# The written order of a decoder layer: output projection and first gate, the slots' steps, the down product's place, and the closing sums

## The chip, the cores and the metric

The kernel runs on one core of one Trainium2 chip. The metric is the device time of one execution in microseconds (us). The kernel before takes 1375.45 us, the median of three executions that lie between 1373.59 and 1375.83. All times below are in us where nothing else is said.

A core has five engines that each run their own queue of instructions in order: TensorE (PE in the profile; PEld is its weight loads), VectorE (DVE), ScalarE (ACT), GpSimd (POOL), and SyncE (SP), which here issues DMA transfers. They wait for each other through semaphores. An instruction that waits holds up everything behind it on its own engine.

## The reference

One post-norm decoder layer on x of 1024 tokens by 1024 columns, all in float32:

```python
mod = silu(c) @ w_mod + b_mod              # shift, scale, gate, twice
h   = x * (1 + scale1) + shift1
mix = hybrid_mixer(h, w_in, w_pool, pool_scale, w_o)
x   = layer_norm(ALPHA * x + gate1 * mix, ln1_g, ln1_b)
h   = x * (1 + scale2) + shift2
ffn = (silu(h @ w_gate) * (h @ w_up)) @ w_down      # D_FF = 2816
x   = layer_norm(ALPHA * x + gate2 * ffn, ln2_g, ln2_b)
```

`hybrid_mixer` projects h, runs eight heads of sparse top-k attention and a causal pooling of 512 channels, sets both beside each other and multiplies by `w_o`. The change touches nothing up to that product. It begins with `... @ w_o`, and reaches to the end: first layer norm, feed-forward part, second layer norm.

## The kernel before, in words

**Split products.** A float32 operand is held as a high half (a copy rounded to the matmul's type fp32r, made by ScalarE) and a low half (the operand less its high half, a subtraction on VectorE or GpSimd). A product is three matmuls, high by high, high by low, and low by high (`SPLITS`). So a matmul may wait for a copy on ScalarE, and the second or third in a row for the subtraction behind it. In the text "low" is that subtraction.

**Output projection.** Tokens stand in eight tiles of 128 (`XR[7]` to `XR[0]`, tiles `res_X` in the trace: tile t at offset 1024*t). For each tile TensorE makes `wo` products, VectorE reads them out onto the residual (`wo_evac`) and takes the statistics of the layer norm, and ScalarE applies it. `region_t(t)` then transposes the tile on TensorE (`xT`), and ScalarE (for the last tiles VectorE in part) applies scale and shift while it copies the transposed blocks to a stage (`stage_W`). Two tiles make one of four regions: region 0 is tiles 7 and 6, region 3 is 1 and 0. `region_sums` makes four differences of blocks per region, T3 on GpSimd, the others on VectorE; `region_split` makes high halves (ScalarE) and low halves (VectorE or GpSimd, `REGION_G`) in `hr_H`, the tokens as the feed-forward products take them. `affine(t)` multiplies the normalized tile by the gain row and adds the bias row on GpSimd, four steps of 128x512, for the residual. In this stage the steps of the four engines are placed by a scheduler from costs; the table `MID` says behind which half of which tile's products each region step is written. From `region_t(2)` on the order is as written ("pinned").

**Feed-forward.** The 2816 columns go in 11 pairs of 256 (`NFP` = 11). Gate, up and down products are each done by a Strassen-like scheme: seven products on 2x2 blocks instead of eight, steps g0 to g6, u0 to u6, d0 to d6. A step is twelve matmuls of 128x512 (`gu` or `dn` in the trace). Its weight block is prepared on GpSimd (`block_prep`: gain products or differences of raw blocks `wraw_R`, `wraw_W`), copied high by ScalarE (`block_high`) and given its low half (`block_low`) by VectorE, or by GpSimd in the slots that `LOW_G` names. There are four block buffers (`wblk_V6144`, `wblk_V7168`, `wblk_T0`, `wblk_T1024`); the copy for the step three ahead is written in this step's slot, its low half one slot later. In the loop over pairs p = 1 to 10 the steps of gate and up of pair p and of down of pair p-1 take turns as `DOWN_AT` says; the last pair has no down steps. The two last pairs' down products are done in a closing part without the scheme.

Up steps end in the product of gate and up, blocks A11 (final after u4), A12, A22 (u6), and from these the differences S1 to S4: `act_W4096` is A11, `act_R2048` is S1, each with high and low half. `utmp_X` and `gtmp_V` hold them in float32. Down steps read them in the order A11, A12, S1, A22, S3, S4, S2; each ends in four sums onto the residual (`res_X<-res_X,dn`) on VectorE.

**What sets the order of a slot.** `slot(sl)` is called once per step, behind the matmuls of step `sl`. It writes, for the step before: the sums and products on VectorE (`prev.vec()`); the lows of block copies (`all_low()`); the lows of activations (`lows`); the differences (`prev.sums()`); preparation of blocks on GpSimd; the copies on ScalarE; and the copy of `sl` itself. Each engine runs its share in this order.

**The end.** The scheme keeps the residual in combined parts; twelve "returns" (`turn`: a sum of two 128x512 parts) undo that in the last pair, on GpSimd but for one (`RETURN_AT`). Behind them stand the gain products of the last two pairs' eight down blocks. Closing: for each tile in `ORDER`, four blocks by three matmuls per half, one sum on VectorE per half, the layer norm, and the output DMA.

All engine calls go through one helper, so nearly every row of the trace shows line L164 of the kernel before (L169 of the changed one); tiles tell the places apart.

## Time and profile before

| | |
|---|---|
| median of three executions | 1375.45 |
| profiled execution, its own time | 1372.83 |
| its span in the trace | 1371.0 |
| mean granted clock of TensorE | 0.938 |
| TensorE matmul busy | 1209.9 (88%) |
| TensorE weight loads busy | 946.9 (69%) |
| VectorE busy | 1055.0 (77%) |
| ScalarE busy | 610.2 (45%) |
| GpSimd busy | 841.3 (61%) |
| DMA, mean over the span | 76 GB/s |

The profiled execution is one execution, not one of the three; span and rows are its own. A row of the timeline or of grouped instructions gives the time from the span's start, the time from the first start to the last end, the engine, the operation, output tiles and input tiles by name, the shape, and the count; in brackets at its end stands the idle time of the engine just before the row and what ended it. The page and the helper leave buffer numbers out of names. Where a mean clock is given it is the share of full speed that TensorE was granted in that stretch.

The stages in the trace: the `wo` products run up to about 640, the first pair's gate and up from there to about 720, then nine pairs with down steps, of which eight are alike, from 722 to about 1270; the last pair and the closing part fill the rest.

### The profile page before, as it was taken

What the parts mean: (1) busy time and instruction counts of PE and PEld (TensorE: products, weight loads), DVE (VectorE), ACT (ScalarE), POOL (GpSimd) and SP (SyncE); (2) the same over time, 40 slices, a digit from 0 to 9 for tenths busy, and PEclk for the clock granted to TensorE, in tenths of its full rate; (3) what the DMA queues carried; (4) which work ended last, traced back from release to release, by engine and by line L of the source; (5) the groups of instructions that cost most, each with busy time, mean ns of one, the idle gap of its engine ahead of it and who ended that gap; (6) DMA issues with size and microseconds to landing.
All of it is one profiled execution on the core that took longest, in us unless ns stands there. A gap on an engine that the chain in (4) does not pass through costs nothing.

```text
span 1371.0 us, 16162 instructions
## 1 busy us (share of the span) xinstructions
PE 1209.9 (88%) x5462; PEld 946.9 (69%) x5462; DVE 1055.0 (77%) x1722; ACT 610.2 (45%) x1149; POOL 841.3 (61%) x790
## 2 busy tenths in 40 slices
PE   7989996778668997997799999999999999999976
PEld 6656575656536654785777787878787787878865
DVE  6898899899988787576687767586777767585678
ACT  3446633545656776346534333343433333342421
POOL 1492774857434456249747767686767767685847
PEclk9999998979869998998999999999999999999988
DMA  9630020301100366400111111201011111202112
GB/s 328 242 139 16 16 92 16 123 16 47 39 16 9 93 207 231 161 24 16 58 58 35 58 62 47 77 31 62 31 63 36 57 62 47 77 32 92 59 50 108
DMA packets 34904, 103.91 MB, mean 76 GB/s; under 512 B 3843, under 2 KB 3843, under 8 KB 33286
## 3 DMA queue, kind: packets, MB, share of 16 engines
q1 hardware_dynamic: 34822, 102.88, 21.7%
q8 instruction: 43, 0.70, 0.2%
q14 instruction: 39, 0.32, 0.1%
HBM read 93.42 MB, written 9.45 MB: 75 GB/s over the span
## 4 chain that ended last, share of the span: by engine, by line
PE 36%; DVE 10%; POOL 3%; issue 2%; ACT 1%; DVEq 0%; POOLq 0%; ACTq 0%
PE gu L164 23%; PE dn L164 14%; DVE utmp_X L164 3%; DVE act_W L164 2%; DVE gtmp_V L164 1%; DVE act_R L164 1%; POOL res_X L164 1%; DVE wblk_T L164 1%; DVE wblk_V L164 1%; POOL wraw_R L164 1%; POOL wraw_W L164 1%; POOL hr_H L164 0%; DVE stat_C L164 0%; DVE res_X L164 0%; DVE hr_H L164 0%
## 5 line engine op out<-in xcount | busy, mean ns | idle before, releaser
L164 PE MATMUL gu<-hr_H,wblk_V 128*128 128x512 f32 (+1 forms) x936 | 225.3, 394 | 15.1 <-DVE wblk_V L164 14.4
L164 PE MATMUL gu<-hr_H,wblk_T 128*128 128x512 f32 (+1 forms) x912 | 218.7, 393 | 11.6 <-DVE wblk_T L164 10.6
L164 PEld LDWEIGHTS gu<-hr_H,wblk_V 128*128 128x128 f32 x936 | 177.1, 193 | 53.9 <-DVE wblk_V L164 16.5
L164 PEld LDWEIGHTS gu<-hr_H,wblk_T 128*128 128x128 f32 x912 | 172.4, 193 | 48.3 <-DVE wblk_T L164 12.3
L164 DVE TENSOR_TENSOR res_X<-res_X,dn 128x512 f32<-128x512 f32 (+1 forms) x253 | 163.5, 680 | 46.1 <-PE dn L164 46.0
L164 PE MATMUL pj<-ws_W,hT_H 128*128 128x512 f32 x456 | 125.5, 425 | 18.7 <-DVE kr_K L164 6.5
L164 PEld LDWEIGHTS pj<-ws_W,hT_H 128*128 128x128 f32 x456 | 89.6, 203 | 46.4 <-issue 16.6
L164 POOL TENSOR_TENSOR wraw_R<-wraw_R 128x512 f32<-128x512 f32 x64 | 93.5, 1467 | 12.9 <-DVE wblk_T L164 6.9
L164 POOL TENSOR_SCALAR sm_H<-sm_H,stat_X 128x1024 f32<-128x1024 f32 (+7 forms) x64 | 58.2, 922 | 70.0 <-DVE stat_X L164 53.4
L164 POOL TENSOR_TENSOR wraw_W<-wraw_W 128x512 f32<-128x512 f32 x60 | 87.9, 1468 | 17.5 <-DVE wblk_T L164 12.9
L164 DVE TENSOR_TENSOR gtmp_V<-gtmp_V,gu 128x512 f32<-128x512 f32 (+1 forms) x47 | 29.7, 650 | 67.7 <-PE gu L164 34.3
L164 PE MATMUL dn<-wblk_T,act_W 128*128 128x512 f32 x336 | 80.8, 392 | 0.0
L164 DVE TENSOR_SCALAR_CACHE_REDUCE junk_X<-keysD_T,colsD_X 128x1024 int16<-128x1024 int16 (+1 forms) x64 | 78.9, 1270 | 0.8
L164 PE MATMUL dn<-wblk_V,act_W 128*128 128x512 f32 x312 | 74.5, 390 | 0.0
L164 PEld LDWEIGHTS dn<-wblk_T,act_W 128*128 128x128 f32 x336 | 64.0, 190 | 13.6
L164 POOL TENSOR_TENSOR wblk_T<-wraw_W,wblk_T 128x512 fp32r<-128x512 f32 x29 | 41.8, 1444 | 44.2 <-ACT wblk_T L164 44.1
L164 PEld LDWEIGHTS dn<-wblk_V,act_W 128*128 128x128 f32 x312 | 58.9, 189 | 12.4
L164 DVE TENSOR_TENSOR utmp_X<-utmp_X,gu 128x512 f32<-128x512 f32 x33 | 22.5, 681 | 57.4 <-ACT utmp_X L164 57.4
L164 POOL TENSOR_TENSOR wblk_T<-wraw_R,wblk_T 128x512 fp32r<-128x512 f32 x29 | 42.4, 1463 | 36.8 <-ACT wblk_T L164 36.5
L164 POOL TENSOR_TENSOR colsA_X<-colsA_X 128x1 f32<-128x1 f32 (+1 forms) x124 | 33.3, 277 | 49.5 <-ACT junkA_T L164 39.0
L164 ACT ACTIVATE wblk_V<-wraw_R 128x512 fp32r<-128x512 f32 x55 | 34.7, 631 | 64.8 <-POOL wraw_R L164 30.4
L164 ACT ACTIVATE wblk_T<-wraw_W 128x512 fp32r<-128x512 f32 x55 | 34.6, 630 | 63.2 <-POOL wraw_W L164 24.0
(300 smaller groups left out, 2873.4 us busy)
## 6 DMA issues: line engine op xcount, KB each, us to landing
wm_K<-in_wma_dram SPq DMA_DIRECT2D x16, 512.0 KB, 10.2
modraw_V<-in_wmc_dram SPq DMA_DIRECT2D x16, 512.0 KB, 4.6
...
```

The lines of the kernel that those rows point to most:

```text
L164: ins_ = f(*a, **k)
```

## The change

One table per decision is changed, and the stage of output projection and first gate is written out by hand.

1. `DOWN_AT` starts a pair with d0 ahead of g0, g1, g2 and ends it with u2 to u6.
2. `slot` takes the order of its three VectorE parts from `SLOT_ORDER` ("b" lows of blocks, "a" lows of activations, "s" differences), and `early` (`COPY_AT`) can put the step's own copy at four places.
3. `LOW_G` names other slots; 46 lows go from GpSimd to VectorE over the kernel. `ACT_G` gives the low of S2 instead of S3 to GpSimd. `FIRST_G` gives the lows of six slots of the first pair to GpSimd.
4. From the first `wo_evac` on the order is as written: readouts and norms of 7, 6, 5 and 4 in turn, each tile's products as a generator (`wo_tile`) between whose halves transposes, differences and splits stand. Of the affine steps those of tiles 4 and 3 go to the slots of the first pair (`mults`, `adds` have ten entries instead of six).
5. The end: six returns are named in the last but one and the last pair and six behind the closing sums of tiles 6 and 5; blocks of the closing part are prepared earlier (`PREP_ON`, `may_make`); for the first two tiles of `ORDER` the half of the closing sums that needs the last but one pair only is written first (`last_down` with `(0, 1)`).

**Boundary of two pairs, TensorE** (one of the steady boundaries; the first row of each list is u6; `wblk` is the weight block, `act_W4096` is A11, `act_W2048` is A12). Before:

```order
L164 MATMUL gu_398_6739<-hr_H0_2677,wblk_V7168_4095 128x512 x12
L164 MATMUL gu_404_6867<-hr_H0_2677,wblk_T0_4096 128x512 x12
L164 MATMUL dn_405_6892<-wblk_T1024_4097,act_W4096_4104 128x512 x3
L164 MATMUL dn_406_6893<-wblk_T1024_4097,act_W4096_4104 128x512 x3
L164 MATMUL dn_407_6894<-wblk_T1024_4097,act_W4096_4104 128x512 x3
L164 MATMUL dn_408_6895<-wblk_T1024_4097,act_W4096_4104 128x512 x3
L164 MATMUL gu_409_6918<-hr_H0_2677,wblk_V6144_4094 128x512 x12
L164 MATMUL gu_404_6867<-hr_H0_2677,wblk_V7168_4095 128x512 x12
```

and now:

```order
L169 MATMUL gu_398_6739<-hr_H0_2677,wblk_V7168_4095 128x512 x12
L169 MATMUL dn_404_6867<-wblk_T0_4096,act_W4096_4104 128x512 x3
L169 MATMUL dn_405_6868<-wblk_T0_4096,act_W4096_4104 128x512 x3
L169 MATMUL dn_406_6869<-wblk_T0_4096,act_W4096_4104 128x512 x3
L169 MATMUL dn_407_6870<-wblk_T0_4096,act_W4096_4104 128x512 x3
L169 MATMUL gu_408_6898<-hr_H0_2677,wblk_T1024_4097 128x512 x12
L169 MATMUL gu_409_6918<-hr_H0_2677,wblk_V6144_4094 128x512 x12
L169 MATMUL gu_408_6898<-hr_H0_2677,wblk_V7168_4095 128x512 x12
```

d0, in both cases four groups of three matmuls on `act_W4096`, now stands right behind u6 (`gu_398` on `wblk_V7168`), ahead of the next pair's g0.

**Same place, VectorE** (from the low half of A11 on). Before:

```order
L164 TENSOR_TENSOR act_W4096_4104<-gtmp_V4096_4111,act_W4096_4104 128x512
L164 TENSOR_TENSOR utmp_X8704_4116<-utmp_X8704_4116,gu_398_6739 128x512
L164 TENSOR_TENSOR gtmp_V4608_4112<-gtmp_V4608_4112,utmp_X8704_4116 128x512
L164 TENSOR_TENSOR act_R2048_4108<-utmp_X8192_4115,act_R2048_4108 128x512
L164 TENSOR_TENSOR utmp_X8192_4115<-utmp_X8192_4115,gtmp_V4096_4111 128x512
L164 TENSOR_TENSOR utmp_X8704_4116<-utmp_X8192_4115,gtmp_V4608_4112 128x512
L164 TENSOR_TENSOR wblk_V7168_4095<-wraw_W0_4103,wblk_V7168_4095 128x512
L164 TENSOR_TENSOR res_X7168_4080<-res_X7168_4080,dn_405_6892 128x512
```

and now:

```order
L169 TENSOR_TENSOR act_W4096_4104<-gtmp_V4096_4111,act_W4096_4104 128x512
L169 TENSOR_TENSOR utmp_X8704_4116<-utmp_X8704_4116,gu_398_6739 128x512
L169 TENSOR_TENSOR gtmp_V4608_4112<-gtmp_V4608_4112,utmp_X8704_4116 128x512
L169 TENSOR_TENSOR wblk_V6144_4094<-wraw_W0_4103,wblk_V6144_4094 128x512
L169 TENSOR_TENSOR act_R2048_4108<-utmp_X8192_4115,act_R2048_4108 128x512
L169 TENSOR_TENSOR utmp_X8192_4115<-utmp_X8192_4115,gtmp_V4096_4111 128x512
L169 TENSOR_TENSOR utmp_X8704_4116<-utmp_X8192_4115,gtmp_V4608_4112 128x512
L169 TENSOR_TENSOR res_X7168_4080<-res_X7168_4080,dn_404_6867 128x512
```

Before, the only block low in this stretch is that of g2 (`wblk_V7168`), behind the low of S1 (`act_R2048`) and the two differences into `utmp_X`; that of g1 was GpSimd's. Now g1's (`wblk_V6144`) is here, ahead of those three, and g2's isn't, and d0's sums (`res_X`) stand directly behind the differences.

**Output projection, GpSimd** (`stage_W4096<-stage_W6144` is region difference T3, `hr_H` the low halves of a region, `res_X` with `gr_G` or `lnb_R` an affine step). Before:

```order
L164 TENSOR_TENSOR res_X6144_4079<-res_X6144_4079,lnb_R2048_4272 128x512
L164 TENSOR_TENSOR hr_H0_2677<-stage_W4096_4092,hr_H0_2677 128x512 x3
L164 TENSOR_TENSOR hr_H0_2677<-stage_W6144_4093,hr_H0_2677 128x512
L164 TENSOR_TENSOR hr_H0_2677<-stage_W4096_4092,hr_H0_2677 128x512
L164 TENSOR_TENSOR res_X5120_4078<-res_X5120_4078,gr_G0_76 128x512 x2
L164 TENSOR_TENSOR res_X5120_4078<-res_X5120_4078,lnb_R2048_4272 128x512 x2
L164 TENSOR_TENSOR res_X4096_4077<-res_X4096_4077,gr_G0_76 128x512 x2
L164 TENSOR_TENSOR res_X4096_4077<-res_X4096_4077,lnb_R2048_4272 128x512 x2
L164 TENSOR_TENSOR stage_W4096_4092<-stage_W6144_4093 128x512
```

and now:

```order
L169 TENSOR_TENSOR stage_W4096_4092<-stage_W6144_4093 128x512
L169 TENSOR_TENSOR hr_H0_2677<-stage_W6144_4093,hr_H0_2677 128x512
L169 TENSOR_TENSOR hr_H0_2677<-stage_W4096_4092,hr_H0_2677 128x512 x4
L169 TENSOR_TENSOR stage_W4096_4092<-stage_W6144_4093 128x512
L169 TENSOR_TENSOR res_X6144_4079<-res_X6144_4079,gr_G0_76 128x512
L169 TENSOR_TENSOR res_X6144_4079<-res_X6144_4079,lnb_R2048_4266 128x512
L169 TENSOR_TENSOR res_X6144_4079<-res_X6144_4079,gr_G0_76 128x512
L169 TENSOR_TENSOR res_X6144_4079<-res_X6144_4079,lnb_R2048_4266 128x512
```

The first T3 in the rows of before is region 1's: it stands behind the affine steps of tiles 5 and 4. In the rows of now the first T3 is region 0's and the second region 1's, which stands ahead of the affine steps of tile 6.

**The end, GpSimd** (`res_X` pairs are returns, `zback` among them; `wraw` with `gr_G` the gain products of the last eight blocks). Before:

```order
L164 TENSOR_TENSOR wblk_T1024_4097<-wraw_W0_4103,wblk_T1024_4097 128x512
L164 TENSOR_TENSOR wraw_R0_4102<-wraw_R0_4102,gr_G0_76 128x512
L164 TENSOR_TENSOR res_X1024_4074<-res_X1024_4074 128x512
L164 TENSOR_TENSOR wblk_V6144_4094<-wraw_W0_4103,wblk_V6144_4094 128x512
L164 TENSOR_TENSOR res_X1024_4074<-res_X1024_4074,zback_W6144_5254 128x512
L164 TENSOR_TENSOR wraw_R0_4102<-wraw_R0_4102,gr_G0_76 128x512 x3
L164 TENSOR_TENSOR wraw_W0_4103<-wraw_W0_4103,gr_G0_76 128x512 x4
```

and now:

```order
L169 TENSOR_TENSOR res_X4096_4077<-res_X4096_4077,res_X5120_4078 128x512
L169 TENSOR_TENSOR res_X5120_4078<-res_X5120_4078 128x512
L169 TENSOR_TENSOR res_X5120_4078<-res_X5120_4078,zback_W6144_5254 128x512
L169 TENSOR_TENSOR res_X3072_4076<-res_X3072_4076,zback_W6144_5254 128x512
L169 TENSOR_TENSOR res_X1024_4074<-res_X1024_4074,zback_W6144_5254 128x512
L169 TENSOR_TENSOR wraw_W0_4103<-wraw_W0_4103 128x512 x4
L169 TENSOR_TENSOR wraw_R0_4102<-wraw_R0_4102,gr_G0_76 128x512 x4
L169 TENSOR_TENSOR wraw_W0_4103<-wraw_W0_4103,gr_G0_76 128x512 x4
```

Before, returns alternate with two lows (`wblk`) up to the gain products. Now the two lows are gone and five of the returns stand together ahead of them; others stand ahead of the rows shown.

The diff, with the rest cut:

```diff
-ACT_G = ("A12", "S3")
-FIRST_G = ()
+ACT_G = ('A12', 'S2')
+FIRST_G = (1, 5, 6, 7, 8, 12)
-MULTS = ("", "", "", "V", "", "VV", "V", "VV", "", "", "", "", "", "")
-ADDS = ("", "", "", "", "", "", "V", "V", "VV", "VV", "", "", "", "")
-RETURN_AT = {"g0": "", "g1": "G", "g2": "G", "g3": "G", "g4": "G", "g5": "G", "g6": "G", "u0": "G", "u1": "G", "u2": "GV", "u3": "G", "u4": "G", "u5": "", "u6": ""}
+MULTS = ('V', '', 'V', '', 'V', 'VG', 'VG', 'G', 'VV', '', '', '', '', '')
+ADDS = ('', '', '', '', '', '', 'V', '', 'VV', 'VG', 'V', 'VV', 'GG', '')
+RETURN_AT = ({"g1": "G", "g2": "G", "g3": "G", "g4": "G"}, {"u5": "G", "u6": "G"})
+SPREAD = 2
+COPY_AT = {'g0': 1, 'g4': 1, 'u0': 2}
+SLOT_ORDER = {'d6': 'sab', 'd2': 'sab', 'g6': 'bsa', 'd3': 'sba', 'u5': 'sba', 'g0': 'sab', 'u6': 'abs', 'd1': 'bsa', 'u2': 'asb', 'g1': 'bsa', 'u1': 'sba'}
+BACK_AT = (6, 5)
+DRAIN_G = False
+PREP_ON = 3
-LOW_G_END = ("u3", "u4")
-LOW_G = ("d2", "d3", "d4", "d6", "g0", "g1", "g6", "u0", "u1", "u4", "u5", "u6")
-DOWN_AT = "gdggdggdgguddduduuuuu"
+LOW_G_END = ()
+LOW_G = ('d4', 'g0', 'g1', 'g4', 'g5', 'u5', 'u6')
+DOWN_AT = 'dgggdggdggddduuduuuuu'
-MID = ((3, 0), (3, 0.5), (3, 1), (2, 0), (2, 0.5), (2, 1), (1, 0), (1, 1))
...
-        return min(len(blocks), pos["used"] + NRING + (4 if pos["used"] >= len(blocks) - 11 else 0))
+        u = pos["used"] - (len(blocks) - 15)
+        return min(len(blocks), pos["used"] + NRING + (min(u, 4) if u > 2 else 0))
...
     def slot(sl, early=False):
         ...
         prev.vec()
-        all_low()
-        for f in lows:
-            f()
-        prev.sums()
-        while pos["prep"] <= may_make() and may_prep():
+        steps = {"b": all_low, "a": lambda: [f() for f in lows], "s": prev.sums}
+        for x in slot_order[0]:
+            steps[x]()
+        while pos["prep"] <= may_make() + prep_on[0] and may_prep():
...
-    for t in (5, 7, 6):
-        for c in range(2):
-            wo_evac(t, c, first[(t, c)])
-    for t in (7, 6, 5):
-        layer_norm_tile(XR[t])
...
-    mid = [lambda: region_t(7), lambda: region_t(6), lambda: (region_sums(0), region_split(0), affine(7)),
-           lambda: (region_t(5), affine(6)), lambda: region_t(4), lambda: (region_sums(1), region_split(1), affine(5)),
-           lambda: (region_t(3), affine(4)), lambda: affine(3)]
-    mid = dict(zip(MID, mid))
-    for t in (4, 3, 2, 1):
+    def wo_tile(t):
...
-            for at in ((t, c), (t, c + 0.5)):
-                if at in mid:
-                    mid[at]()
+            yield
-        if t > 1:
-            layer_norm_tile(XR[t])
-        if t == 2:
-            load_set(0)
+    def norm(t):
+        return layer_norm_tile(XR[t], later=True)
     pinned.update("TVAG")
-    region_t(2)
+    for t in (7, 6):
+        for c in range(2):
+            wo_evac(t, c, first[(t, c)])
+        norm(t)()
+    for c in range(2):
+        wo_evac(5, c, first[(5, c)])
+    wo = wo_tile(4)
+    next(wo)
+    next(wo)
+    next(wo, None)
+    region_t(7)
+    norm(5)()
+    wo = wo_tile(3)
+    next(wo)
+    region_t(6)
+    n4 = norm(4)
+    affine(7)
+    region_sums(0)
+    n4()
+    next(wo)
+    region_split(0, (B22,))
+    region_t(5)
+    region_split(0, (B11, T3, T2, B21, T1, T4))
+    next(wo, None)
+    norm(3)()
+    wo = wo_tile(2)
+    next(wo)
+    region_t(4)
+    region_sums(1)
+    affine(6)
+    next(wo)
+    region_split(1)
+    next(wo, None)
+    load_set(0)
+    norm(2)()
+    region_t(3)
+    affine(5)
+    wo = wo_tile(1)
+    next(wo)
+    next(wo)
+    next(wo, None)
...
-    mults = [(1, 1), (1, 0), (2, 0), (2, 1), (0, 0), (0, 1)]
+    mults = [(3, 1), (3, 0), (4, 1), (4, 0), (1, 1), (1, 0), (2, 0), (2, 1), (0, 0), (0, 1)]
...
+    def back(eng):
+        z, x = turn.pop(0)
+        eng.tensor_tensor(z, z, x, ALU.add)
+            slot_order[0] = SLOT_ORDER.get(kind + str(n), "bas")
+            prep_on[0] = PREP_ON if p == NFP - 1 and kind == "u" and n > 1 else 0
...
-            for e in RETURN_AT[kind + str(n)] if p == NFP - 1 else ():
-                z, x = turn.pop(0)
-                (G if e == "G" else V).tensor_tensor(z, z, x, ALU.add)
+            for e in RETURN_AT[NFP - 1 - p].get(kind + str(n), "") if p >= NFP - 2 else ():
+                back(G if e == "G" else V)
...
+    def last_down(pp, t, c0, c1, qs):
+        c = c0 // 512
+        for q in qs:
+            wd_ = block(pos["used"] + 4 * (q // 2) + 2 * c + q % 2)
+            for m, (a, b) in enumerate(SPLITS):
+                T.matmul(pp, act_op(acts[2 * q : 2 * q + 2], a, t), wd_[:, b * 512 + c0 % 512 : b * 512 + c0 % 512 + c1 - c0],
+                         start=(q == 0 and m == 0), stop=(q == 3 and m == 2))
+    begun = {(t, c0): psA("dn") for t in ORDER[0:SPREAD] for c0 in (0, 512)}
+    for (t, c0), pp in begun.items():
+        last_down(pp, t, c0, c0 + 512, (0, 1))
     for t in ORDER:
         ...
-            c, n = c0 // 512, c1 - c0
-            pp = psA("dn")[:, 0:n]
-            for q in range(4):
-                ...
+            if (t, c0) in begun:
+                pp = begun[(t, c0)]
+                last_down(pp, t, c0, c1, (2, 3))
+            else:
+                pp = psA("dn")[:, 0 : c1 - c0]
+                last_down(pp, t, c0, c1, range(4))
             ...
+            if t in BACK_AT and c0 == 0:
+                for _ in range(3):
+                    back(G)

```

More of the change, by code (lines that the diff above doesn't have):

```diff
@@ L1514, in slot @@
             block_high()
+        if early == 2:
+            sl.copy()
         for f in highs:
             f()
+        if early == 3:
+            sl.copy()
         prev.act()
@@ L1614, in decoder_layer_kernel @@
     wo_last(1, 0, 2)
+    region_t(2)
     block_prep()
@@ L1682, in decoder_layer_kernel @@
         low_by[0] = n in FIRST_G
-        slot(gu_step("g", n, 2, 2, None) if n < 7 else gu_step("u", n - 7, 0, 4, ACTS), n < EARLY)
+        slot(gu_step("g", n, 2, 2, None) if n < 7 else gu_step("u", n - 7, 0, 4, ACTS), 1 if n < EARLY else COPY_AT.get(f"u{n - 7}", 0))
         for e in MULTS[n]:
```

23 lines of the change are left out of this document (8 added, 15 removed).

## Prediction

> **What bounds the kernel now.** I began with the busy time per stage (columns: stretch, its length, then busy time and count for TensorE, weight loads, VectorE, ScalarE, GpSimd; clock, DMA share, GB/s).
>
> ```profile
> 620.00:640.00 20.00, 11.67 (x56) 9.43 (x54) 11.61 (x22) 10.80 (x27) 19.26 (x15) 0.87 0.04 14
> 1092.36:1153.93 61.57, 58.92 (x253) 48.31 (x253) 43.63 (x57) 22.30 (x38) 43.48 (x31) 0.97 0.15 52
> 1270.88:1312.74 41.86, 33.29 (x147) 27.14 (x146) 24.15 (x24) 18.60 (x35) 37.23 (x26) 0.93 0.15 51
> ```
>
> TensorE is almost always busy, DMA almost never; so the time is TensorE's work, its gaps, and its half clock behind gaps. Both orders hold the same matmuls, so only gaps and clock can change. The first row is the output projection: TensorE busy 11.67 of 20, clock 0.87, GpSimd 19.26. The last is the last pair, 33.29 of 41.86. The one between is a steady pair of feed-forward columns: 61.57. A step of twelve matmuls starts 2.72 after the last (below), 21 steps are 57.12, so a steady pair loses 4.5. The timeline of TensorE at the boundary of two pairs shows where:
>
> ```profile
> 1139.79 5.60 PE L164 MATMUL gu<-hr_H,wblk_V 128*128 128x512 f32 x24
> 1145.23 2.88 PE L164 MATMUL dn<-wblk_T,act_W 128*128 128x512 f32 x12
> 1147.95 2.88 PE L164 MATMUL gu<-hr_H,wblk_T 128*128 128x512 f32 x12
> 1150.67 0.61 PE L164 MATMUL gu<-hr_H,wblk_V 128*128 128x512 f32 x2
> 1153.93 3.98 PE L164 MATMUL gu<-hr_H,wblk_V 128*128 128x512 f32 x10 [2.65 <-DVE wblk_V L164]
> ```
>
> These are u6 with g0, then d0, g1, and g2, which after two matmuls waits 2.65 for VectorE's low half of its weight block. VectorE meanwhile:
>
> ```profile
> 1139.99 0.69 DVE L164 TENSOR_TENSOR gtmp_V<-gtmp_V,gu 128x512 f32<-128x512 f32 x1 [0.33 <-PE gu L164]
> 1140.71 0.69 DVE L164 TENSOR_TENSOR utmp_X<-gtmp_V,gtmp_V 128x512 f32<-128x512 f32 x1
> 1141.32 2.38 DVE L164 TENSOR_TENSOR act_W<-gtmp_V,act_W 128x512 fp32r<-128x512 f32 x2
> 1147.02 1.79 DVE L164 TENSOR_TENSOR act_R<-utmp_X,act_R 128x512 fp32r<-128x512 f32 x1
> 1148.85 3.35 DVE L164 TENSOR_TENSOR utmp_X<-utmp_X,gtmp_V 128x512 f32<-128x512 f32 x2
> 1152.12 1.75 DVE L164 TENSOR_TENSOR wblk_V<-wraw_R,wblk_V 128x512 fp32r<-128x512 f32 x1
> ```
>
> It never rests: that low stands eleventh after u5 and lands 13.9 after it. A step costs 0.6 from start to start when its second input is PSUM or GpSimd is quiet, 1.7 beside a GpSimd step; GpSimd's goes from 1.25 to 1.7:
>
> ```profile
> 1097.51 0.68 DVE L164 TENSOR_TENSOR wblk_T<-wraw_W,wblk_T 128x512 fp32r<-128x512 f32 x1
> 1098.12 2.47 DVE L164 TENSOR_TENSOR res_X<-res_X,dn 128x512 f32<-128x512 f32 x4
> 1124.61 1.29 POOL L164 TENSOR_TENSOR wblk_V<-wraw_W,wblk_V 128x512 fp32r<-128x512 f32 x1
> 1140.78 1.77 POOL L164 TENSOR_TENSOR wraw_R<-wraw_R 128x512 f32<-128x512 f32 x1
> ```
>
> After the gap the granted clock is half for some 3.3, which costs the other 1.6 or so; after gaps of about 1 it is not:
>
> ```profile
> 1094.00:1095.00 1.00, 1.00 (x4) 0.79 (x3) 1.00 (x3) 0.10 (x1) 0.92 (x2) 0.50 0.00 0
> 1096.00:1097.00 1.00, 1.00 (x6) 0.81 (x5) 1.00 (x2) 0.50 (x2) 0.44 (x1) 1.00 0.00 0
> 687.33 1.70 PE L164 MATMUL gu<-hr_H,wblk_W 128*128 128x256 f32 x12 [1.25 <-ACT gtmp_V L164]
> 688.00:690.00 2.00, 1.83 (x15) 1.62 (x14) 2.00 (x5) 0.82 (x3) 1.04 (x1) 1.00 0.06 12
> ```
>
> **The change, part by part.**
>
> *C, the steady boundary (eight times).* t counts from the first VectorE row above. TensorE now runs u6, d0, g0, g1, g2, d1. d0's third matmul, nominally at t=2.97, reads A11's low, which is still fourth on VectorE. GpSimd holds only one step there, since its next (S2's difference) waits for g1's low; so A11's low ends at 3.7 as the `act_W` row says, and d0 waits 0.8. Bounds: 0 with GpSimd quiet (0.7+3×0.6=2.5), 2.9 if all three are held (0.7+3×1.7=5.8). g1's low now stands eighth, ahead of S1's low and the two differences, with GpSimd idle: 3.7+4×0.6+0.1=6.2, needed at 9.2. No wait. Behind it GpSimd runs S2's difference, a gain product, A12's low and g2's low: 6.2 plus four steps of 1.25 to 1.7, with ScalarE's copy of A12 (behind two others) in between, 11.7 to 12.6, needed at 11.9: 0 to 0.7, I take 0.4. g3's low, after d0's four sums and S3's and S4's lows, comes near 16.6, needed near 17.9. So 1.2 a boundary, in two gaps below 1.25 each and so without half clock, against 4.5: 3.3 × 8 = 26.6. With both bounds high the boundary costs 2.9+0.7+1.6 = 5.2, no gain; with both low 0, a gain of 36. I stay near the middle because the `act_W` row is the very step that decides. In the rest of the pair, lows moved from GpSimd to VectorE (46 over the kernel) fall where VectorE waits, as before d6's sums:
>
> ```profile
> 1127.07 2.73 DVE L164 TENSOR_TENSOR res_X<-res_X,dn 128x512 f32<-128x512 f32 x4 [2.44 <-PE dn L164]
> 1136.54 0.69 DVE L164 TENSOR_TENSOR utmp_X<-utmp_X,gu 128x512 f32<-128x512 f32 x1 [5.54 <-ACT utmp_X L164]
> ```
>
> Five more a pair are 3.0 alone, 8.5 if all are held; 16 of idle time cover that (18 less the boundary's 2). The Trainium skill, "SBUF — State Buffer", section "Who interferes with whom", speaks against this move: it says a VectorE step with two SBUF inputs and a GpSimd step that reads SBUF exclude each other for the whole instruction. The 0.6 and 1.7 above agree; by the rule alone, with every moved step held, VectorE would get 46 × 1.1 = 51 longer, an estimate, but under that idle time the sum stays.
>
> *B, the first boundary.* Same walk, except that d0's sums are ScalarE copies. Before, it loses 3.8, and 1.4 and 0.5 of half clock:
>
> ```profile
> 722.40 3.70 PE L164 MATMUL gu<-hr_H,wblk_V 128*128 128x512 f32 x10 [3.82 <-DVE wblk_V L164]
> 725.90 3.40 PE L164 MATMUL dn<-wblk_T,act_W 128*128 128x512 f32 x12
> ```
>
> 5.8−1.2 = 4.6 (0 to 5.8). The reload of the gain row stands a slot later behind one more product on VectorE; GpSimd idled 9.8 for it without holding TensorE, and d0 comes one slot sooner: nothing, or 3 if that cover is gone.
>
> *A, output projection and first gate.* The largest gap:
>
> ```profile
> 628.79 2.88 PE L164 MATMUL wo<-hr_H,plT_T 128*128 128x512 f32 x12
> 641.20 1.97 PE L164 MATMUL xT<-const_C,res_X 128*128 128x128 f32 x8 [9.53 <-ACT res_X L164]
> 655.74 3.04 PE L164 MATMUL gu<-hr_H,wblk_V 128*128 128x256 f32 x24
> 666.77 1.12 PE L164 MATMUL xT<-const_C,res_X 128*128 128x128 f32 x4 [3.02 <-DVE stage_W L164]
> 625.31 3.45 POOL L164 TENSOR_TENSOR res_X<-res_X,gr_G 128x512 f32<-128x512 f32 x2
> 632.11 1.27 POOL L164 TENSOR_TENSOR stage_W<-stage_W 128x512 f32<-128x512 f32 x1
> 635.11 0.82 DVE L164 TENSOR_TENSOR hr_H<-stage_W,hr_H 128x512 fp32r<-128x512 f32 x1 [2.91 <-ACT hr_H L164]
> 637.41 2.45 DVE L164 TENSOR_SCALAR stat_C<-stat_C 128x1 f32<-128x1 f32 x11
> 639.90 1.24 ACT L164 ACTIVATE res_X<-res_X,stat_C 128x1024 f32<-128x1024 f32 x1 [2.56 <-DVE stat_C L164]
> ```
>
> A difference on GpSimd stands behind eight affine products, ScalarE's splits wait for it, VectorE's split for those, and tile 2's norm, whose matmuls were done by 620, behind that. In the written order the difference precedes its affine, and tiles 4 and 3 lose theirs here (eight GpSimd steps; they go to the slots after). A tile costs VectorE 5.15 (639.78 for the next tile, less 635.86, plus two readouts). Walked from 581.0: norms 7, 6 at 586.2, 591.3; 5, 4 at 599.2, 603.2; three differences, two splits and norm 3 at 618.9; the next three and two and norm 2 at 631 to 633; norm 1 at 636.9 to 638.6. ScalarE's norm and eight stage copies (1.25 and 2.85) follow each. TensorE, unhindered, wants tiles 3, 2, 1 at 620.05, 636.0, 639.7 and gets 620 to 621, in time, 641.2 to 642.3. First gate matmul: 646 to 647.5 instead of 655.74. Behind it VectorE is later relative to TensorE than before (three differences and three splits stand right ahead of tile 0), so the second half of tile 0's transposes comes at 657.3 to 659 instead of 666.77. 8.5 is kept; bounds 0 (the chain through tile 0 unchanged) and 19 (all gaps of this stage gone, summed from the timeline). ScalarE's waits behind 667 are left as they are.
>
> *D, the end.*
>
> ```profile
> 1303.77 0.39 PE L164 MATMUL dn<-hr_H,act_R 128*128 128x512 f32 x1
> 1312.74 1.22 PE L164 MATMUL dn<-hr_H,act_R 128*128 128x512 f32 x2 [8.57 <-DVE hr_H L164]
> 1358.12 0.52 PE L164 MATMUL dn<-wblk_V,hr_H 128*128 128x256 f32 x3
> 1301.38 3.76 POOL L164 TENSOR_TENSOR wraw_R<-wraw_R,gr_G 128x512 f32<-128x512 f32 x3
> 1305.10 5.83 POOL L164 TENSOR_TENSOR wraw_W<-wraw_W,gr_G 128x512 f32<-128x512 f32 x4
> ```
>
> From u6's end (1304.0) to TensorE's end (1358.6) are 54.6; 192 matmuls of 0.227 are 43.5. The gap is GpSimd's last eight products, queued behind ten returns of residual parts. In the new order six returns stand ahead of or around the last boundary, two lows leave GpSimd, and the products are released two to three slots sooner: 20 steps in the 38 that fourteen slots give, so they end about u6's end, and 24 matmuls (5.4) that need only the previous pair's results run first. I take 0.5 left: 10 (bounds 2, if GpSimd still ends 3 late and the clock halves, and 11). The 12.4 from TensorE's end to the end of the span stay.
>
> Sum: 26.6+4.6+8.5+10 = 49.7. The profiled execution took 1372.83 (span 1371.0), 2.6 below the median of 1375.45, 0.2%: 1323.1 by its scale, up to 1326 by the median's. I say **1324**.
>
> **Rivals.** (1) *VectorE's queue still binds*: GpSimd meets every step, A11's low ends at 5.8, the boundary costs 4 to 5 with half clock. For it: 1.7 in most rows above; against: GpSimd waits there for g1's low. B and C go: 1372.8−18.5 = 1354. (2) *The short gaps cool the clock too*: +1.6 × 9: 1338. Against: 1.25 with clock 1.00; the Trainium skill, "TensorE: Matmul & The Clock Gate", Part 1, puts cooling at an idle window of about 3.4, in free-running windows. By that even 2.65 would cool only sometimes; the row shows it, so the measurement decides and this rival keeps a chance. (3) *Everything hides*: C 36, B 5.8, A 8.5, D 11: 1312. Needs GpSimd to miss VectorE at A22's and A11's lows, against the 2.38 row. (4) *Slower*: "down first" moves A11's low onto the path with no step of cover. If it and g2's low are each 2.9 late and each gap halves the clock, a boundary costs 9.0: 9×4.5 = 40 more, less 18.5: 1394. It decides from 6.6 a boundary, where A and D are used up; nothing shows two such waits. (5) *Not as written*: four of the six returns put into the closing sums stand before the last boundary instead. They cost 5 to 7 of GpSimd time after d6's sums, where it idled 5.8 and 2.3: at worst 1326.
>
> **How the numbers follow.** Forecast 0.55, (1) 0.15, (2) 0.10, (3) 0.13, (4) 0.03, (5) 0.04. Forecast alone: 1314 to 1334. To leave out no more than 0.2 I go to 1309 and 1346. Below 0.2% this measurement tells no change; between forecast and (4) almost nothing lies there: faster 0.95, same 0.02, slower 0.03.
>
> **What would show it.** Steady pair 58.3 long, with a gap of about 0.8 in d0 behind VectorE's `act_W` and a smaller one in g2 behind GpSimd; clock 1.00 throughout. First 256-wide gate matmul near 647; no gap above 2 between u6's end and the last sum. Wrong if d0 waits over 2, if the clock is half at each boundary, or if a new gap stands at d3 to d5 or u1 to u4, where lows moved to VectorE.

## The result

The changed kernel takes 1338.34 us, the median of four executions between 1337.45 and 1338.67; the kernel before, run beside it, takes 1375.06 (1373.59 to 1375.83). The ratio is 0.9733, 95% interval 0.9716 to 0.9750. It is faster, and the time lies in the range of 1309 to 1346, but 14 above the forecast of 1324. Some seven tenths of the forecast gain came.

The profiled executions show where. Their spans are 1371.0 and 1335.7, so 35.3 are to be divided. The stages are cut where TensorE begins or ends the same step in both traces: the last up step of the first pair ends at 709.80 and now at 706.85; the second feed-forward pair begins at 772.65 and 768.59; the last pair at 1265.49 and 1239.49.

| stage | before | after | gain | forecast |
|---|---|---|---|---|
| A: up to the first pair's u6 | 709.80 | 706.85 | 2.95 | 8.5 |
| B: first pair with a boundary | 62.85 | 61.74 | 1.1 | 4.6 |
| C: eight steady pairs | 492.84 | 470.90 | 21.9 | 26.6 |
| D: last pair and closing | 105.51 | 96.21 | 9.3 | 10 |

All four terms came out below the forecast, so no miss hid another; that the time is in the range is owed to the range's width.

TensorE's timeline in the changed kernel at one steady boundary, with the busy row of that pair (window row: length, busy time and count of TensorE, weight loads, VectorE, ScalarE, GpSimd, then clock):

```profile
1180.65 0.61 PE L169 MATMUL dn<-wblk_T,act_W 128*128 128x512 f32 x2
1181.90 2.58 PE L169 MATMUL dn<-wblk_T,act_W 128*128 128x512 f32 x10 [0.63 <-DVE act_W L169]
1184.32 2.88 PE L169 MATMUL gu<-hr_H,wblk_T 128*128 128x512 f32 x12
1187.04 3.33 PE L169 MATMUL gu<-hr_H,wblk_V 128*128 128x512 f32 x14
1190.84 2.57 PE L169 MATMUL gu<-hr_H,wblk_V 128*128 128x512 f32 x10 [0.47 <-POOL wblk_V L169]
1193.24 2.88 PE L169 MATMUL dn<-wblk_T,act_W 128*128 128x512 f32 x12
...
1123.06:1181.90 58.84, 57.74 (x253) 47.15 (x253) 44.57 (x62) 21.55 (x38) 36.47 (x25) 1.00 0.16 54
```

d0 stands behind u6 and waits 0.63 for the low half of A11; g2 waits 0.47 for a low of GpSimd's; the clock is 1.00. Both waits are where the prediction put them (0.8 and 0.4), and they are alike at all eight boundaries, but for one 0.85 in d0. But a wait costs more than its idle time. d0's twelve matmuls take 3.67 from the first start at 1180.65 to the next step at 1184.32, against 2.72 for a step without a wait: 0.95 for an idle time of 0.63. g1 and g2 take 6.20 against 5.44: 0.76 for 0.47. Together 1.7, which is the pair's 58.84 less 57.12. About half of what is beyond the idle time is how a row counts: the two matmuls ahead of d0's wait have 0.61 of busy time, though two starts are 0.45 apart, so the idle time begins 0.16 late; the other half is that the ten matmuls behind it take 2.42 instead of 2.27. In the pair's busy times, VectorE has five steps more than before and only 0.94 more busy time; GpSimd has six less, 36.47 against 43.48.

TensorE's timeline of the changed kernel in stage A, and the first boundary:

```profile
643.52 1.97 PE L169 MATMUL xT<-const_C,res_X 128*128 128x128 f32 x8 [3.35 <-ACT res_X L169]
645.14 6.37 PE L169 MATMUL wo<-hr_H,plT_T 128*128 128x512 f32 x18
651.35 3.04 PE L169 MATMUL gu<-hr_H,wblk_V 128*128 128x256 f32 x24
659.35 0.83 PE L169 MATMUL xT<-const_C,res_X 128*128 128x128 f32 x4 [2.81 <-ACT res_X L169]
663.02 1.12 PE L169 MATMUL xT<-const_C,res_X 128*128 128x128 f32 x4 [2.84 <-DVE stage_W L169]
709.52 3.49 PE L169 MATMUL dn<-wblk_T,act_W 128*128 128x512 f32 x10 [2.06 <-DVE act_W L169]
```

The gap of 9.53 is gone and one of 3.35 stands in its place, with half clock behind it (eighteen matmuls in 6.37). The first gate matmul is at 651.35 (before 655.74, forecast near 647), the second half of tile 0's transposes at 663.02 (before 666.77, forecast 657.3 to 659). The first d0 waits 2.06, not 0.8.

The half clock there isn't part of the new order. In spread0 (below), whose order up to the closing part is the changed kernel's, the same wait of 3.35 stands there and the clock behind it is 1.00:

```profile
642.76 1.09 PE L169 MATMUL xT<-const_C,res_X 128*128 128x128 f32 x8 [3.35 <-ACT res_X L169]
647.83 3.03 PE L169 MATMUL gu<-hr_H,wblk_V 128*128 128x256 f32 x24
```

The first gate matmul stands at 647.83 there, and at 647.65 in first13, close to the forecast. The second half of tile 0's transposes is at 662.54 and 662.36, no more than 0.7 earlier than in the changed kernel: the 3.5 that the clock costs at the gate steps are gone before it.

The end, from the last pair's g2 on:

```profile
1246.60 2.56 PE L169 MATMUL gu<-hr_H,wblk_V 128*128 128x512 f32 x10 [1.06 <-DVE wblk_V L169]
1282.34 3.47 PE L169 MATMUL dn<-hr_H,act_W 128*128 128x512 f32 x14 [0.99 <-DVE hr_H L169]
```

The 8.57 are gone; 0.99 is left, and a wait of 1.06 in the last pair is new.

### The profile page after: what moved, and what is told of

It is laid out like the page before. It is cut to its first block, busy times and chain, and to the rows that moved or that the text cites. A ratio compares the mean times of both kernels' runs of the same rounds, so it can differ in the third digit from the quotient of the medians.

```text
span 1335.7 us, 16132 instructions
## 1 busy us (share of the span) xinstructions
PE 1197.2 (90%) x5462; PEld 932.9 (70%) x5462; DVE 1071.7 (80%) x1769; ACT 604.0 (45%) x1149; POOL 780.7 (58%) x743
## 4 chain that ended last, share of the span: by engine, by line
PE 38%; DVE 6%; POOL 4%; issue 2%; ACT 1%; DVEq 0%; POOLq 0%; ACTq 0%
PE gu L169 24%; PE dn L169 14%; DVE act_W L169 2%; POOL wraw_R L169 1%; DVE utmp_X L169 1%; POOL wraw_W L169 1%; DVE gtmp_V L169 1%; POOL wblk_T L169 0%; DVE wblk_T L169 0%; DVE hr_H L169 0%; POOL hr_H L169 0%; DVE res_X L169 0%; DVE stat_C L169 0%; POOL wblk_V L169 0%; DVE wblk_V L169 0%
## 5 line engine op out<-in xcount | busy, mean ns | idle before, releaser
L169 PE MATMUL gu<-hr_H,wblk_V 128*128 128x512 f32 (+1 forms) x924 | 215.2, 384 | 3.7 <-POOL wblk_V L169 1.9
L169 PE MATMUL gu<-hr_H,wblk_T 128*128 128x512 f32 (+1 forms) x924 | 215.8, 385 | 2.9 <-POOL wblk_T L169 1.9
L169 PEld LDWEIGHTS gu<-hr_H,wblk_V 128*128 128x128 f32 x924 | 170.1, 188 | 40.0 <-POOL wblk_V L169 3.6
L169 DVE TENSOR_TENSOR res_X<-res_X,dn 128x512 f32<-128x512 f32 (+1 forms) x253 | 159.0, 680 | 15.4 <-PE dn L169 15.3
L169 PE MATMUL dn<-wblk_V,act_W 128*128 128x512 f32 x324 | 78.5, 391 | 2.9 <-DVE act_W L169 2.5
L169 PEld LDWEIGHTS dn<-wblk_T,act_W 128*128 128x128 f32 x324 | 60.9, 189 | 19.5 <-DVE act_W L169 6.9
L169 ACT ACTIVATE wblk_V<-wraw_W 128x512 fp32r<-128x512 f32 x53 | 33.1, 627 | 75.1 <-POOL wraw_W L169 56.5
L169 ACT ACTIVATE wblk_T<-wraw_R 128x512 fp32r<-128x512 f32 x52 | 32.5, 627 | 61.0 <-POOL wraw_R L169 45.6
L169 POOL TENSOR_TENSOR ws_W<-raw_R,ws_W 128x1024 fp32r<-128x1024 f32 x11 | 29.9, 2721 | 51.3 <-ACT ws_W L169 51.3
L169 ACT ACTIVATE sm_H<-sm_H,stat_X 128x1024 f32<-128x1024 f32 (+7 forms) x64 | 49.0, 768 | 18.5 <-DVE stat_X L169 15.5
```

The lines of the kernel that those rows point to most:

```text
L169: ins_ = f(*a, **k)
```

## The experiments

All kernels were timed beside the kernel before. Its medians there were 1373.5, 1373.9, 1376.9 and 1374.3, so ratios compare better than microseconds; intervals are 95%, and a difference of less than about 2 between two of these kernels is not told from none.

### The loop alone, and the new place of the down steps alone

```diff
 (loop_only, against the kernel before)
+LOW_G, ACT_G, DOWN_AT, SLOT_ORDER, COPY_AT and the code in slot() that reads them, as changed,
+for pairs 1 to 9; everything else as before
 (down_only, against the kernel before)
-DOWN_AT = "gdggdggdgguddduduuuuu"
+DOWN_AT = 'dgggdggdggddduuduuuuu'
```

> The kernel before with the tables of the steady loop alone (place of the down steps, order of the slot's VectorE parts, which lows go to GpSimd, early copies); output projection, first pair and end stay as before. Theory 'the parts add up': by the two traces the nine boundaries gave 23.0 (8 x 2.83 and 0.5 at the first one), so 1375 - 23 = 1352, with a steady pair of 58.8 and waits of 0.63 in d0 and 0.47 in g2. Rival 'the parts need each other': the rest of the pair or the last pair loses something that the other parts had covered, and the time is 1357 or more. By the prediction's own terms (31.2) it would be 1344.

> The kernel before with the new place of the down steps alone. Theory 'the boundary is all': in the slots of d0 and u6 the old order of VectorE's parts puts the same steps ahead of A11's low and of g1's low, so the waits at the boundary are those of the whole change (0.63 and 0.47) and the time is 1352 to 1356. Rival 'the order of steps carries it': somewhere else in the pair lows or sums now come late, the pair is over 60 long, and the time is 1362 or more.

Measured: loop_only 1351.06, ratio 0.9839 (0.9816 to 0.9862); down_only 1358.33, ratio 0.9889 (0.9869 to 0.9909). The first is the expected 1352: its 22.4 less than the kernel before are close to the 23.0 that B and C show in the whole change. No run has A or D alone. The second lies between its two theories. Its timeline has d0's wait nearly unchanged, and another behind it:

```profile
772.68 2.56 PE L164 MATMUL dn<-wblk_T,act_W 128*128 128x512 f32 x10 [0.67 <-DVE act_W L164]
785.03 2.79 PE L164 MATMUL dn<-wblk_T,act_W 128*128 128x512 f32 x11 [0.90 <-POOL wblk_T L164]
832.46 2.58 PE L164 MATMUL dn<-wblk_V,act_W 128*128 128x512 f32 x10 [0.67 <-DVE act_W L164]
```

The pair is 59.78 long (832.46 - 772.68). Moving the down product accounts for some two thirds of what the loop gains; the rest is order and engine of the lows and sums and the early copies, which no run parts.

### The old choice of GpSimd's lows

```diff
-LOW_G = ('d4', 'g0', 'g1', 'g4', 'g5', 'u5', 'u6')
+LOW_G = ("d2", "d3", "d4", "d6", "g0", "g1", "g6", "u0", "u1", "u4", "u5", "u6")
-ACT_G = ('A12', 'S2')
+ACT_G = ("A12", "S3")
```

> The changed kernel with the old choice of which lows GpSimd makes (blocks in the loop and S3 instead of S2), all else as changed. Theory of the prediction 'cover': lows on VectorE fall where it waits; moved back they cost GpSimd some 5 x 1.45 = 7 a pair where it idles about 15 of 58.8, and TensorE sees little of it: 1338 to 1342. Rival 'GpSimd's queue binds': the lows stand ahead of a block that TensorE waits for, a new gap of 1 or more a pair: 1347 or more.

Measured: 1358.16, ratio 0.9885 (0.9870 to 0.9900). The rival holds, though for one low alone. TensorE's timeline, and GpSimd's ahead of one of these waits:

```profile
840.75 2.60 PE L169 MATMUL gu<-hr_H,wblk_T 128*128 128x512 f32 x10 [2.19 <-POOL wblk_T L169]
901.37 4.14 PE L169 MATMUL gu<-hr_H,wblk_V 128*128 128x512 f32 x10 [2.19 <-POOL wblk_V L169]
```

```profile
1138.98 1.67 POOL L169 TENSOR_TENSOR wraw_R<-wraw_R 128x512 f32<-128x512 f32 x1 [3.76 <-DVE wblk_T L169]
1140.61 1.74 POOL L169 TENSOR_TENSOR wraw_W<-wraw_W,gr_G 128x512 f32<-128x512 f32 x1
1142.32 1.74 POOL L169 TENSOR_TENSOR act_W<-utmp_X,act_W 128x512 fp32r<-128x512 f32 x1
1144.03 1.28 POOL L169 TENSOR_TENSOR act_W<-gtmp_V,act_W 128x512 fp32r<-128x512 f32 x1
1145.27 1.74 POOL L169 TENSOR_TENSOR wblk_V<-wraw_R,wblk_V 128x512 fp32r<-128x512 f32 x1
```

After g1's low (the wait of 3.76) GpSimd makes a difference of raw weight blocks (the prediction's "S2's difference"), a gain product, S3's low (`act_W<-utmp_X`, 1.74), A12's low, and only then g2's. S3's low is the one step that the changed kernel doesn't have there, and g2 waits 2.19 instead of 0.47 at every boundary. A pair without half clock is 60.6 long, 1.7 more than the change's 58.84, just that step; with 1.5 of half clock at four of the eight boundaries (last section) that makes 8 x 1.7 + 4 x 1.5 = 20, the whole difference. So the block lows that went back to GpSimd, five a pair, cost TensorE nothing that can be seen, and the activation low cost everything. This is read from the trace; no run moves that one low alone.

### One chain through two queues

Three exchanges, each undoing the wait that the one ahead of it left:

```diff
 (a11_first: u6's slot makes A11's low ahead of A22's, on VectorE)
-'u6': 'abs'
+'u6': 'Abs'          # "A": the activation lows in reverse
 (g2_first: g0's slot makes g2's low ahead of A12's, on GpSimd)
-'g0': 'sab'
+'g0': 'sba'
 (both_lows: both of these;  g1_early: both, and)
+        if slot_order[0][0] == "B":     # d0's slot: g1's low ahead of u6's two steps on VectorE
+            all_low()
         prev.vec()
```

> The changed kernel with the two activation lows of the u6 slot exchanged, so that A11's low comes ahead of A22's (which d3 needs, much later). Theory 'A11's low is late by its place': it ends 0.6 earlier (at about 1181.2 instead of 1181.84 at the last boundary), the wait of 0.63 in d0 goes at eight boundaries, and with the 0.3 that a gap costs beyond its idle time a pair gets 0.6 to 0.95 shorter: 1331 to 1334. Rival 'something else ends that wait' (the weight block, or a GpSimd step that holds VectorE's first low whatever it is): 1337 to 1339.

> The changed kernel with one exchange on GpSimd: in the slot of g0 the low of g2's block stands ahead of A12's low, not behind it (the order of VectorE is untouched). Theory 'two waits, one chain each': g2's low ends 1.6 earlier, at about 1189.1 in the clock of the changed kernel's trace, where TensorE wants it at 1189.76; the wait of 0.47 goes and with it 0.76 a pair, d0's 0.63 stays: pair 58.1, 1338 - 8 x 0.76 = 1332. Rival 'A12 is late instead': d1, which now follows A12's low closely, waits as long: 1337 to 1339.

> Both exchanges together: A11's low ahead of A22's on VectorE, and g2's low ahead of A12's on GpSimd. Theory 'the wait moved': A11's exchange alone brought 1 because the 0.6 that it freed in d0 came back in g2, whose low hangs on g1's low and three GpSimd steps and not on TensorE; with that low 1.6 earlier both waits go and a pair comes to 57.1 to 57.4: 1338 - 8 x 1.6 = 1325, up to 1327. Rival 'VectorE's queue bounds the pair': another wait (d1, g3 or d3) takes the place of the two: 1331 or more.

> Both exchanges and a third: in the slot of d0 the low of g1's block stands ahead of u6's two products on VectorE, not behind them. Theory 'one chain through two queues': with both exchanges the wait had moved once more, to d1, whose block's low is fifth on GpSimd behind g1's low; that low 1.3 earlier moves the five GpSimd steps with it, d1's low ends near 1186.6 in the trace of both exchanges, where d1 wants it at 1187.56, and a pair comes from 58.24 to 57.4 to 57.7: 1333 - 8 x 0.55 to 0.85 = 1326 to 1329. Rival 'the pair is bound elsewhere': 1332 to 1334, with the wait at yet another step.

| kernel | median | ratio (95%) | wait in d0 | in g2 | in d1 | in g3 | pair |
|---|---|---|---|---|---|---|---|
| changed | 1338.34 | 0.9733 (0.9716 to 0.9750) | 0.63 | 0.47 | | | 58.84 |
| a11_first | 1337.08 | 0.9733 (0.9718 to 0.9747) | | 1.08 | | | 58.83 |
| g2_first | 1333.35 | 0.9699 (0.9683 to 0.9715) | 0.63 | | | | 58.26 |
| both_lows | 1332.91 | 0.9698 (0.9684 to 0.9712) | | | 0.20 | | 58.24 |
| g1_early | 1346.48 | 0.9779 (0.9752 to 0.9806) | | | | 1.29 | 59.90 |

(Waits under 0.15 left out; 0.39 in a later d step of g1_early too.) The first exchange does what it should to d0 and nothing to the time: the 0.6 comes back in g2. Its timeline:

```profile
1190.31 2.56 PE L169 MATMUL gu<-hr_H,wblk_V 128*128 128x512 f32 x10 [1.09 <-POOL wblk_V L169]
```

So d0's wait was not on the chain that sets the pair. That chain runs from u5's end through eight VectorE steps to g1's low, from there through GpSimd to g2's low, and it takes the same time whether TensorE waits ahead of it or not. Shortening it by one GpSimd step (g2_first) brings 5, close to the 6 expected. Doing both brings no more than the second alone; the wait goes on to d1, whose low is fifth in the same GpSimd queue.

The third exchange was to start that queue 1.3 earlier. It did, d1's wait is gone, and the kernel is 14 slower by the medians, 11 by the ratios, 15 by the profiled spans. VectorE of both_lows (first fence) and of g1_early (second), from the lows of A11 and A22 on, with the pair's busy row:

```profile
1174.83 2.38 DVE L169 TENSOR_TENSOR act_W<-gtmp_V,act_W 128x512 fp32r<-128x512 f32 x2
1179.05 0.68 DVE L169 TENSOR_TENSOR wblk_V<-wraw_W,wblk_V 128x512 fp32r<-128x512 f32 x1
1179.65 0.68 DVE L169 TENSOR_TENSOR act_R<-utmp_X,act_R 128x512 fp32r<-128x512 f32 x1
...
896.49:954.73 58.24, 58.04 (x253) 46.92 (x253) 45.02 (x62) 21.50 (x38) 36.27 (x26) 1.00 0.16 55
```

```profile
1188.17 2.38 DVE L169 TENSOR_TENSOR act_W<-gtmp_V,act_W 128x512 fp32r<-128x512 f32 x2
1191.08 0.68 DVE L169 TENSOR_TENSOR wblk_V<-wraw_W,wblk_V 128x512 fp32r<-128x512 f32 x1
1192.39 1.28 DVE L169 TENSOR_TENSOR gtmp_V<-gtmp_V,utmp_X 128x512 f32<-128x512 f32 x1
1193.60 1.77 DVE L169 TENSOR_TENSOR act_R<-utmp_X,act_R 128x512 fp32r<-128x512 f32 x1
...
1085.41:1145.31 59.90, 58.18 (x252) 46.98 (x252) 49.17 (x62) 22.01 (x38) 37.22 (x26) 1.00 0.15 53
```

And TensorE of g1_early at g3:

```profile
1205.19 2.56 PE L169 MATMUL gu<-hr_H,wblk_T 128*128 128x512 f32 x10 [1.29 <-DVE wblk_T L169]
```

The same 62 VectorE steps a pair take 49.17 instead of 45.02. While GpSimd waited for g1's low, VectorE's next steps ran at 0.6 from start to start; with GpSimd started earlier they meet its steps and take up to 1.77, and g3's low, further down VectorE's queue, becomes the bound. The stretch in which GpSimd is idle was not waste; it is when VectorE is fast.

### The first boundary

```diff
-FIRST_G = (1, 5, 6, 7, 8, 12)
+FIRST_G = (1, 5, 6, 7, 8, 12, 13)
```

> The changed kernel with the two block lows of the first pair's last slot on GpSimd instead of VectorE. Theory 'the first boundary waits for two lows that the others don't have there': A11's low ends 1.2 earlier, the wait of 2.06 in the first d0 falls to 0.9 or less, the half clock behind it goes: 2 to 3 less, 1335 to 1336. Rival 'GpSimd holds VectorE's lows the longer': 1338.

Measured: 1339.29, ratio 0.9743 (0.9729 to 0.9758): nothing. VectorE there in the changed kernel and in first13:

```profile
705.92 0.68 DVE L169 TENSOR_TENSOR wblk_T<-wraw_R,wblk_T 128x512 fp32r<-128x512 f32 x1
706.52 0.68 DVE L169 TENSOR_TENSOR wblk_T<-wraw_W,wblk_T 128x512 fp32r<-128x512 f32 x1
707.12 2.35 DVE L169 TENSOR_TENSOR act_W<-gtmp_V,act_W 128x512 fp32r<-128x512 f32 x2
```

```profile
706.40 3.44 DVE L169 TENSOR_TENSOR act_W<-gtmp_V,act_W 128x512 fp32r<-128x512 f32 x2
```

The two block lows are indeed there, 1.2 ahead of A11's. On GpSimd they and the difference behind them hold the two activation lows instead, 3.44 for both. The first d0 still waits 1.76, and g2 waits 0.4 and 0.2. These two waits aren't owed to the edit: spread0 and t4_early, which leave `FIRST_G` as changed, have 1.81 in the first d0 and the same 0.4 and 0.2 in g2. In all three the clock is full behind d0's wait, so g2 comes sooner than in the changed kernel.

### Output projection

```diff
 (t4_early: tile 4's transposes and their copies ahead of tile 3's norm on ScalarE)
-    norm(3)()
     wo = wo_tile(2)
     next(wo)
+    n3 = norm(3)
     region_t(4)
+    n3()
 (t0_early: that, and two of region 2's splits behind tile 0's statistics)
-    region_split(2, (B11, T3, B21, T4))
+    region_split(2, (B11, T3))
     ...
     norm0 = layer_norm_tile(XR[0], later=True)
+    region_split(2, (B21, T4))
```

> The changed kernel with ScalarE's copies of tile 4's transposes ahead of tile 3's norm instead of behind it (in the changed trace they wait for that norm from 614.5 to 620.0, and VectorE's differences wait 2.77 for them). Theory 'ScalarE's order is what A lacked': the differences start at about 618.9, tile 2's and tile 1's norms come 2.7 earlier, the wait of 3.35 ahead of tile 1's transposes falls under 1 and the 2.3 of half clock behind it go, the first gate matmul stands near 646 instead of 651.35, and 3 to 5 of it reach the end: 1333 to 1335. Rival 'tile 0's chain sets the end of this stage': the first gate matmul comes earlier, but the transposes of tile 0 do not: 1337 to 1339.

> Tile 4's copies ahead of tile 3's norm, and two of the three low halves of region 2 that stand ahead of tile 0's readout on VectorE put behind tile 0's statistics. Theory 'tile 0's chain sets the end of this stage': its readout comes 1.4 to 2.7 earlier (from 649.65 to 647 or 648), the transposes of tile 0 as much, and the time is 1334 to 1335.5. Rival 'the first gate steps wait for the halves that now come late' or a later chain sets the end: 1336.5 or more.

Measured: t4_early 1336.62, ratio 0.9725 (0.9710 to 0.9739); t0_early 1336.85, ratio 0.9714 (0.9688 to 0.9741). First, ScalarE of the changed kernel around tile 3's norm, and VectorE's wait for it:

```profile
618.90 1.25 ACT L169 ACTIVATE res_X<-res_X,stat_C 128x1024 f32<-128x1024 f32 x1 [5.07 <-DVE stat_C L169]
620.04 2.88 ACT L169 ACTIVATE stage_W<-xT,const_C 128x128 f32<-128x128 f32 x8
```

```profile
621.64 1.39 DVE L169 TENSOR_TENSOR stage_W<-stage_W 128x512 f32<-128x512 f32 x1 [2.77 <-ACT stage_W L169]
623.06 3.38 DVE L169 TENSOR_TENSOR stage_W<-stage_W,stage_W 128x512 f32<-128x512 f32 x2
626.36 3.48 DVE L169 TENSOR_TENSOR hr_H<-stage_W,hr_H 128x512 fp32r<-128x512 f32 x2
```

Then TensorE and VectorE of t4_early:

```profile
640.91 1.09 PE L169 MATMUL xT<-const_C,res_X 128*128 128x128 f32 x8 [1.46 <-ACT res_X L169]
645.95 3.03 PE L169 MATMUL gu<-hr_H,wblk_V 128*128 128x256 f32 x24
660.69 1.11 PE L169 MATMUL xT<-const_C,res_X 128*128 128x128 f32 x4 [2.14 <-DVE stage_W L169]
```

```profile
645.65 4.08 DVE L169 TENSOR_TENSOR hr_H<-stage_W,hr_H 128x512 fp32r<-128x512 f32 x3
649.65 1.27 DVE L169 SCALAR_TENSOR_TENSOR res_X<-res_X,wo 128x512 f32<-128x512 f32 x2
```

The copies waited behind a norm that wasn't ready. With them moved the first gate matmul stands at 645.95, as expected, 5.4 before the changed kernel's; but 3.5 of that is the half clock, which spread0 and first13 don't have there either. Against spread0 the gate is 1.9 earlier, tile 0's readout 1.85 (649.65, there 651.50), and the second half of tile 0's transposes 1.85 (660.69, there 662.54). So the order brings some 1.9, and all of it reaches the transposes. The spans differ by 1.8, the times by a bare 1.7, too little to be told from none. In t0_early tile 0's readout is another 3.8 earlier (645.86), and nothing more is gained: ScalarE makes tile 0's norm at 656.32, in t4_early at 656.61, because a weight copy ahead of it waited for the splits that had been moved.

```profile
654.74 0.63 ACT L169 ACTIVATE wblk_W<-wraw_R 128x512 fp32r<-128x512 f32 x1 [3.91 <-DVE hr_H L169]
656.32 1.23 ACT L169 ACTIVATE res_X<-res_X,stat_C 128x1024 f32<-128x1024 f32 x1
```

### The closing sums

```diff
-SPREAD = 2
+SPREAD = 0
```

> The changed kernel without the 24 closing matmuls written ahead (each closing sum whole in its place); earlier preparation and returns stay. Theory of the prediction, term D: those 5.4 of work cover the last lows of blocks, which come near 1282 to 1287 where TensorE would want the first at 1280.3; without them it waits 4 to 5, perhaps with half clock behind it: 1342 to 1346. Rival 'the earlier products and the moved returns alone gave the gain': 1338 to 1340.

Measured: 1343.78, ratio 0.9765 (0.9734 to 0.9795), the profiled span 2.6 longer than that of the change. The two larger waits at the start of the closing part are these; one of 0.23 follows:

```profile
1281.30 0.49 PE L169 MATMUL dn<-wblk_V,hr_H 128*128 128x512 f32 x1 [0.73 <-ACT hr_H L169]
1283.05 0.50 PE L169 MATMUL dn<-wblk_V,hr_H 128*128 128x512 f32 x1 [1.25 <-DVE wblk_V L169]
```

The 24 matmuls written ahead are worth 2.6 by the spans, of which 1.8 lies between the last up step and TensorE's last matmul, and 4.4 by the ratios, whose intervals overlap. The direction agrees with the theory, the size isn't settled. What is left of D, the larger part, comes with the earlier products on GpSimd:

```profile
1272.92 6.41 POOL L169 TENSOR_TENSOR wraw_W<-wraw_W,gr_G 128x512 f32<-128x512 f32 x4
```

In the changed kernel they end at 1279.33, 0.4 behind the last up step; before, they ended at 1310.9, some 7 behind it. This part is found by subtraction: no run leaves out the moved returns and lows or the earlier preparation.

### What paid, together

```diff
 both_lows and t4_early
```

> Both exchanges of lows, and tile 4's copies ahead of tile 3's norm: the edits of this study that shortened the profiled span, together. Theory 'they stand in different stages and add': 1332.9 - 1.7 = 1331, ratio near 0.968, spans 1328 to 1329. Rival 'the stage's gain is given back at the first boundary': 1333 or more, ratio 0.970.

Measured: 1332.16, ratio 0.9697 (0.9676 to 0.9717). It is faster than the kernel before and than the change, whose interval (0.9716 to 0.9750) it touches at its edge; it is not told from both_lows alone. That tile 4's copies add anything is not shown.

## Why the prediction was right, and where it was off

**The bound.** Matmuls unchanged, gaps and clock less: right. TensorE's busy time fell from 1209.9 to 1197.2 for the same 5462 matmuls, by the clock (0.938 to 0.953).

**C.** The place of both waits and their sizes (0.63 for 0.8, 0.47 for 0.4) came out of the walk through the queues, and the clock held at 1.00. The term failed by its price for a wait, which it took as the idle time alone: 1.1 of idle time cost 1.7, because at each wait about 0.3 goes in addition (rows at 1180.65 and 1187.04). That is 0.5 a pair of the 0.6 that were missing. The step "lows moved from GpSimd to VectorE fall where VectorE waits" held: lows_old puts them back and no other wait in a pair than g2's grows by more than 0.1. The other exchange of the same table, S2's low for S3's on GpSimd, had no term of its own, though the walk contained it (S3's low does not stand ahead of g2's there); by lows_old it was worth some 20.

Adding both waits up as two savings still to be had would have failed as well: a11_first shows that one of them was no saving at all.

**B.** "Same walk" was the step that failed. The first pair's last slot makes two block lows on VectorE ahead of A11's that GpSimd makes elsewhere, and the order of parts there is the default. The wait was 2.06 with half clock behind it, not 0.8: at this one boundary the prediction's own sign of being wrong, a d0 that waits over 2, came. (Over the other runs with this boundary it is 1.8 to 2.2, with and without half clock.) That the two lows are the cause is only half shown: they stand there, but moving them off changed nothing, because GpSimd then held VectorE as long. The cause stays open.

**A.** The largest miss, 2.95 for 8.5. It isn't the first gate matmul: without the half clock it comes within 1 of the forecast 647. It is tile 0's chain, whose transposes were forecast at 657.3 to 659 and came at 663.02 (662.4 and 662.5 without the half clock). The first step that failed is that ScalarE's norm and eight stage copies follow each: in the written order tile 4's copies stand behind tile 3's norm, and region 1's differences came 2.8 late for it. t4_early mends this, and some 1.9 reaches tile 0. The second is the price of VectorE's steps beside GpSimd, which stayed when the first was mended: the two differences took 3.38, two splits 3.48, three splits 4.08, two to three times what undisturbed ones take. How much of the rest that is, no run shows. The bound of 0 that the prediction named, "the chain through tile 0 unchanged", was the closer end.

**D.** 9.3 for 10. GpSimd's products ended 0.4 behind u6, as forecast. The last pair lost 1.35 of TensorE's time, where before it lost 0.2, at a wait that no term held (1.06 in g2); closing sums and tail gave 10.4 together.

**The rivals.** Rival (2), that short gaps cool the clock, named 1338, which is the measured time; it is not what happened. In the changed kernel's profile the clock is 1.00 behind every wait of 0.4 to 1.1, and of the missing 14.4 by the spans 9 lie in A and B (5.5 and 3.5) and 4.7 in C. A number that fits is no evidence for its mechanism. Rival (1), VectorE's queue at 1354, did not come, but its mechanism is what g1_early brought about: GpSimd meeting every VectorE step. Rival (4), slower, had d0 and g2 wait 2.9 each; they waited 0.6 and 0.5. Rival (5) was so: the four returns run on GpSimd from 1226.17 to 1232.57, and GpSimd waited 2.16 for ScalarE behind them, so they cost nothing that can be seen.
